# Queries and keys of an attention stage rotated by pairs of heads, transposed raw and split into high and low afterwards, with three of the four query pairs moved into the attention loop

## The chip, the cores and the metric

The kernel runs on one core of a Trainium2 chip. Five engines work side by side, each from its own queue and in the order of that queue: TensorE (PE in the profile; its weight loads are PEld), VectorE (DVE), ScalarE (ACT), GpSimd (POOL) and SyncE (SP), which only starts transfers. An engine that needs something from another waits on a semaphore, and everything behind the waiting instruction in its queue waits with it. The metric is the device time of one execution in microseconds (us).

## The reference

The reference is one encoder layer in float32, applied to two sequences of 512 tokens and 1024 channels. Each sequence goes through a feed-forward half step, a mixing block, and a second feed-forward half step. What matters here is the attention within the mixing block: 8 query heads of 64 channels share 2 key and value heads. Queries and keys are normalized per head, rotated by position in pairs of neighbouring channels, and used for a full softmax over the 512 tokens.

```python
aq = apply_rope(rms_norm(aq.reshape(B, S, ATT_HEADS, ATT_HEAD_DIM), q_norm), cos, sin)
ak = apply_rope(rms_norm(ak.reshape(B, S, ATT_KV_HEADS, ATT_HEAD_DIM), k_norm), cos, sin)

def apply_rope(x, cos, sin):
    x0, x1 = xf[..., 0], xf[..., 1]
    out = jnp.stack([x0 * c - x1 * s, x0 * s + x1 * c], axis=-1)

s = jnp.einsum('bqkgd,bskd->bkgqs', qi, k) * scale
p = jax.nn.softmax(s, axis=-1)
o = jnp.einsum('bkgqs,bskd->bqkgd', p, v)
```

Beside the attention the block computes a bidirectional chunkwise mLSTM memory and several sigmoid gates, all from one input projection.

## The kernel before

**High and low.** Every matmul works on pairs of float32r tiles: a value x is split into a high part (a copy rounded by ACT) and a low part (x minus the high part, by DVE). A projection is then three products (high by high, high by low, low by high). An attention score of one head over 64 channels is two products: the query tile holds the 64 high rows in one half of the 128 partitions and the 64 low rows in the other, and the key tile holds the high rows twice for the first product and the low rows twice for the second.

**The mixing block** is the generator `mix(s, ...)`, run once for each sequence, s = 0 and s = 1; the steps of the two are interleaved. In the profiled execution the part before the attention of s = 0 ends near 710 us and its attention loop lies at 710 to 830 us; the part before the attention of s = 1 is at 1020 to 1065 us and its loop at about 1090 to 1200 us. Tiles are tokens by channels until they are transposed: 4 blocks of 128 tokens stand side by side in a 128 x 512 tile.

**Before the attention.** `kv_done` normalizes and rotates the keys (`rope_apply`, L823 on: a product with the inverse root n, a product with the cosines o, products of the swapped neighbours with the sines m, and the sum). It splits them into `kst`, and `k_turn` transposes `kst` in 4 groups of 4 blocks. `q_done` leaves the raw queries of the 4 token blocks in four tiles. `q_rope(b)` does one token block with all its 8 heads: 4 DVE operations of 128 x 512, the split in two halves, 8 transposes of 128 x 128, and ACT copies into `qT` (heads by tokens). All four token blocks are done before the loop.

**The attention loop** (from L1112) runs over the heads h = 0 to 7 and, within a head, over b = 0 to 3. One step (h, b) puts on PE: the score of the next head for query block b (`score`, 2 matmuls); 5 filler matmuls of the gate projections (`among(FILLER[0])`); `turn_keys(Ps, b)`, which transposes key block b of the four probability tiles (4 transposes); 3 more filler matmuls; and `values` for the step before (2 matmuls). For each score DVE takes the row maximum (L1042), ACT the exponential (L1044), DVE the reciprocal (L1045), and either engine scales the tile (L1049 on DVE, L1047 on ACT). For each `turn_keys` ACT copies the high part out of PSUM and DVE forms the low part (`split`, L673 and L674); DVE's low part is the last reader of that bank.

**PSUM.** `PT()` hands out the two banks that the names pst belong to, in turn. Every transposing group of the mixing block takes one: `turn_keys`, the statistics of the other sequence (`col_sums`, L202, and its spreading, L212), and the turns of keys and queries. A group can start only when the last reader of the group two before it is done. Scores use two other banks (pss), fillers three (mm), values one (pso).

**Order.** Instructions wrapped in `pin` keep the order in which they are written; this holds for the scores, the transposes and values of the loop and for its fillers. All others are placed by a scheduling layer, and `shifted(n)` moves them in its order. While s = 0 runs, weights are fetched and split by ACT and DVE (`split_w`, L238 and L239, 128 x 1024 each) and also stored; for s = 1 they are loaded already split. The gate projections that serve as fillers end in a DVE product with the spread inverse root and an ACT tanh (`att_gate`, L1100 and L1101; `out_gate`, L974 and on).

Of the kernel before, what the change touches and what calls it, by code (L numbers as in the profile page):

```python
# [26 lines left out]
def encoder(ctx, tc, I, outs):  # L27
# [768 lines left out]
    def mix(s, xh, xl, early=None, extra=None, after=None):  # L796
# [26 lines left out]
        def rope_apply(t, rq, tab, bsel):  # L823

            cg, sg = tab
            if bsel is None:
                nb, cb, sb = 4, cg.unsqueeze(2).to_broadcast([P, 4, 2, DA]), sg
            else:
                nb, cb, sb = 1, cg[:, bsel].unsqueeze(1).to_broadcast([P, 8, DA]).unsqueeze(1), sg[:, bsel:bsel + 1]
            hn_ = 8 // nb  # L830
            n = T2()
            V_.tensor_tensor(n.rearrange("p (h e) -> p h e", e=DA), t.rearrange("p (h e) -> p h e", e=DA),
                             rq.unsqueeze(2).to_broadcast([P, 8, DA]), op=ALU.mult)
            o, m = T2(), T2()
            v4 = lambda x: x.rearrange("p (b h e) -> p b h e", b=nb, e=DA)
            V_.tensor_tensor(v4(o), v4(n), cb, op=ALU.mult)
            v5 = lambda x: x.rearrange("p (b h i two) -> p b h i two", b=nb, h=hn_, two=2)
            s4 = sb.rearrange("p b (i two) -> p b i two", two=2)
            for bb in range(nb):
                V_.tensor_tensor(v5(m)[:, bb], v5(n)[:, bb, :, :, ::-1],  # L840
                                 s4[:, bb].unsqueeze(1).to_broadcast([P, hn_, DA // 2, 2]), op=ALU.mult)
            V_.tensor_tensor(o, o, m, op=ALU.add)
            return o

        qT = A([P, HA, S], F32R, "qT")
        kst = qT[:, 4:8, :].rearrange("p a (g j u e) -> p (a g) j u e", g=2, j=2, u=2)

        def kv_done(pk):
# [10 lines left out]
            ko = rope_apply(kraw, rstd_cols(ssk, 8, DA), tabs[1], None)  # L859
            ko3 = ko.rearrange("p (g e) -> p g e", e=DA)  # L860
            nc.scalar.activation(kst[:, :, 0, 0, :], ko3, AF.Copy)
            nc.scalar.activation(kst[:, :, 0, 1, :], ko3, AF.Copy)
            V_.tensor_tensor(kst[:, :, 1, 0, :], ko3, f(kst[:, :, 0, 0, :]), op=ALU.subtract)
            V_.tensor_tensor(kst[:, :, 1, 1, :], ko3, f(kst[:, :, 0, 1, :]), op=ALU.subtract)

        qraw, rq = [], []

# [238 lines left out]
        if not s:  # L1106
            fill(1)
# [680 lines left out]
```

## Time and profile before

| | |
|---|---|
| three runs, median | 2062.38 us (2060.41, 2062.38, 2063.18) |
| span of the profiled execution, first to last instruction | 2059.1 us |
| granted TensorE clock, mean | 0.999 |
| PE busy | 2047.3 us, 99% |
| PE weight loads busy | 1691.3 us, 82% |
| DVE busy | 1553.0 us, 75% |
| ACT busy | 913.0 us, 44% |
| POOL busy | 92.8 us, 5% |
| chain of work that ended last | PE 97%, DVE 1%, ACT 1%, DMA 1% |

Of the profiled execution only the span is given, 3.3 us below the median of the three runs; no total time of its own stands beside it. A row of the timeline reads: start, duration, engine, line, operation, tile written <- tiles read, shape, how often, and in brackets the idle time of that engine before it with what ended it. Several like instructions in a row share a line (x2, x8). A duration on DVE or ACT is longer than the distance to the next start, since neighbours overlap a little: 128 x 512 operations of DVE last 0.69 us and start every 0.60 us when nothing holds them.

### The profile page before, as it was taken

How to read it: one execution, taken by the hardware profiler on the slowest of the kernel's cores; microseconds unless marked ns; L12 is line 12 of the kernel's file. 1: busy time of each engine (PE TensorE's matmuls, PEld its weight loads, DVE VectorE, ACT ScalarE, POOL GpSimd, SP SyncE). 2: the span in 40 equal slices, each digit the busy share in tenths (PEclk: the TensorE clock that was granted, in tenths of full speed). 3: DMA queues.
4: the chain of work that ended last, by engine and by line, in shares of the span. 5: the costliest groups of instructions: out<-in, count | busy, mean ns of one | idle time of the engine just before them, and what ended most of it. 6: DMA issues, size and time to landing. Idle time of an engine off the chain costs nothing.

```text
span 2059.1 us, 27038 instructions
## 1 busy us (share of the span) xinstructions
PE 2047.3 (99%) x9445; PEld 1691.3 (82%) x9445; DVE 1553.0 (75%) x2764; ACT 913.0 (44%) x1667; POOL 92.8 (5%) x108
## 2 busy tenths in 40 slices
PE   9999999999999999999999999999999999999998
PEld 7888888888888888888888888888888888888887
DVE  8888889886797787675566756455788888796797
ACT  7544444442235567563334553324544444443224
POOL 0000000001003000100120000001000000000001
PEclk9999999999999999999999999999999999999999
DMA  9656556799766753877684345677656555599753
GB/s 321 198 170 221 177 191 205 243 349 348 260 227 247 223 187 130 278 259 242 197 310 160 109 140 200 196 265 239 202 175 202 194 174 184 186 342 347 276 202 119
DMA packets 311015, 457.97 MB, mean 222 GB/s; under 512 B 20232, under 2 KB 182112, under 8 KB 309600
## 3 DMA queue, kind: packets, MB, share of 16 engines
q1 hardware_dynamic: 308800, 450.27, 64.6%
q0 software_dynamic: 1920, 5.72, 0.9%
q8 instruction: 74, 1.21, 0.2%
q14 instruction: 61, 0.50, 0.1%
q10 hardware_dynamic: 160, 0.27, 0.0%
HBM read 288.25 MB, written 167.94 MB: 222 GB/s over the span
## 4 chain that ended last, share of the span: by engine, by line
PE 97%; DVE 1%; ACT 1%; DMA 1%; issue 0%; SPq 0%; ACTq 0%; DVEq 0%
PE mm L789 15%; PE pso L332 12%; PE pst L332 12%; PE mm L332 10%; PE mm L590 8%; PE pss L332 6%; PE mm L776 6%; PE pst L590 4%; PE pss L590 4%; PE mm L756 4%; PE pso L590 3%; PE pso L1066 1%; PE pss L1039 1%; PE pst L1055 1%; PE pso L1235 1%; PE pss L1185 1%
## 5 line engine op out<-in xcount | busy, mean ns | idle before, releaser
L332 PE MATMUL pst<-xc,w 128*128 128x512 f32 x1056 | 253.6, 389 | 0.0
L332 PEld LDWEIGHTS pst<-xc,w 128*128 128x128 f32 x1056 | 198.3, 188 | 41.1
L332 PE MATMUL mm<-xc,w 128*128 128x512 f32 x972 | 229.9, 390 | 0.2 <-ACT f L340 0.2
L332 PEld LDWEIGHTS mm<-xc,w 128*128 128x128 f32 x972 | 181.9, 188 | 38.1 <-ACT f L340 0.6
L590 PE MATMUL mm<-rt,w 128*128 128x512 f32 x765 | 178.9, 389 | 0.0
L789 PE MATMUL mm<-xh,w 128*128 128x512 f32 x560 | 177.6, 393 | 0.0
L590 PEld LDWEIGHTS mm<-rt,w 128*128 128x128 f32 x765 | 143.6, 188 | 29.8
L290 ACT ACTIVATE w<-t 128x512 fp32r<-128x512 f32 x176 | 106.5, 627 | 135.7 <-issue 63.1
L291 DVE TENSOR_TENSOR w<-t,w 128x512 fp32r<-128x512 f32 x176 | 117.8, 688 | 47.9 <-ACT w L290 46.6
L332 PE MATMUL pss<-xc,w 128*128 128x512 f32 x528 | 126.8, 389 | 0.0
L332 PE MATMUL pso<-xc,w 128*128 128x512 f32 x528 | 126.8, 389 | 0.0
L332 PE MATMUL pso<-xc,f 128*128 128x512 f32 x528 | 126.8, 389 | 0.0
L789 PEld LDWEIGHTS mm<-xh,w 128*128 128x128 f32 x560 | 104.7, 188 | 21.2 <-DVE w L239 0.2
L332 PEld LDWEIGHTS pss<-xc,w 128*128 128x128 f32 x528 | 99.2, 188 | 20.5
L332 PEld LDWEIGHTS pso<-xc,w 128*128 128x128 f32 x528 | 99.1, 188 | 20.5
L332 PEld LDWEIGHTS pso<-xc,f 128*128 128x128 f32 x528 | 99.1, 188 | 20.5
L776 PE MATMUL mm<-xh,w 128*128 128x512 f32 x336 | 114.5, 401 | 0.0
L789 PE MATMUL mm<-xl,w 128*128 128x512 f32 x280 | 109.7, 392 | 0.0
L673 ACT ACTIVATE w<-wr 128x512 fp32r<-128x512 f32 x72 | 45.1, 632 | 137.0 <-PE pso L590 71.4
L673 ACT ACTIVATE w<-t 128x512 fp32r<-128x512 f32 x82 | 51.8, 632 | 107.4 <-PE pst L590 62.4
L590 PE MATMUL pst<-rt,w 128*128 128x512 f32 x396 | 93.7, 389 | 0.0
L590 PE MATMUL pss<-rt,w 128*128 128x512 f32 x396 | 93.7, 389 | 0.0
(407 smaller groups left out, 4037.5 us busy)
## 6 DMA issues: line engine op xcount, KB each, us to landing
rt<-rbuf SPq DMA_DIRECT2D x154, 512.0 KB, 5.7
wpark<-w SPq DMA_DIRECT2D x104, 512.0 KB, 3.4
w<-wpark SPq DMA_DIRECT2D x104, 512.0 KB, 4.8
wr<-in_ffn_w_gate_dram SPq DMA_DIRECT2D x62, 512.0 KB, 5.3
rbuf<-tab SPq DMA_DIRECT2D x102, 256.0 KB, 3.9
wr<-in_ffn_w_up_dram SPq DMA_DIRECT2D x44, 512.0 KB, 4.5
rbuf<-f SPq DMA_DIRECT2D x72, 256.0 KB, 4.1
wr<-in_w_in_dram SPq DMA_DIRECT2D x36, 512.0 KB, 5.7
```

Source lines behind the costliest of these rows:

```text
L290: pin(nc.scalar.activation(t[:, 0], src, AF.Copy))
L291: pin(V_.tensor_tensor(t[:, 1], src, f(t[:, 0]), op=ALU.subtract))
L332: nc.tensor.matmul(p, a[:, k, :], xt[:, b, k, :], start=(first and k == 0 and i == 0), stop=(k == HK_ - 1 and i == 2), skip_group_check=True)
L590: nc.tensor.matmul(p, u[:, a, d * P:(d + 1) * P], r[:, b, ts], start=(first and q == 0 and k == 0), stop=(q == len(us) - 1 and k == 2), sk ...
L673: nc.scalar.activation(hi, src, AF.Copy)
L756: nc.tensor.matmul(p[b][:, :N], a[:, k, bs], w_[:, kl, :], start=(k == 0 and i == 0), stop=(k == KD - 1 and i == 2))
L776: pin(nc.tensor.matmul(p[0], a[:, k, :], b, start=(k == 0 and i == 0), stop=(k == n - 1 and i == 2)))
L789: nc.tensor.matmul(p, a[:, k, :], b, start=(k == 0 and i == 0), stop=(k == n - 1 and i == 2))
L1039: pin(nc.tensor.matmul(p, qT[:, h, b * P:(b + 1) * P], kv[:, hk * 2 + j, :], start=(j == 0), stop=(j == 1)))
L1055: pin(nc.tensor.transpose(p[:, b * P:(b + 1) * P], Ps[b][:, kb * P:(kb + 1) * P], ident))
L1066: pin(nc.tensor.matmul(pos[h], Vst[:, kb, h // 4, :], w, start=(kb == 0 and i == 0), stop=(kb == 3 and i == 1)))
L1185: nc.tensor.matmul(p, qk[a][:, isl], qk[b], start=(n == 0), stop=(n == 2))
```

## The change

The rotation now works on a pair of heads for all four token blocks at once (a tile of 4 blocks by 128 channels). The pair is transposed as it is, unsplit, in one group of 4 (`pair_turn`), which gives both heads' 64 channels on the two halves of the partitions with all 512 tokens. The split comes after that, out of PSUM: for each head ACT copies the high half and DVE writes the low half to the other partitions, 64 x 512 each. For the keys one such group serves both heads. `kst`, its copies and its low parts go, and so do the splits of the queries in front of their transposes.

Per sequence PE transposes 4 blocks for the keys instead of 16, and 16 for the queries instead of 32. Over both sequences PE has 56 matmul instructions fewer (9377 for 9433), ACT 20 activations fewer, DVE 8 tensor operations more: the product with the sines is now two instructions of 256 columns in place of one of 512. Transfers and POOL's instructions are the same in number.

Query pair 1 (heads 0 and 1) is done before the loop. Pairs 2 to 4 are rotated at the loop's steps (0,0), (2,0) and (3,2) and turned at (0,2), (2,2) and (4,2), there pinned after the values and ahead of the next score. The raw queries wait in the upper half of `mg`, the tile that later takes the gates of the attention; the gates 4 to 7 of `att_gate` therefore come after the two `out_gate` units. `gate_tops` comes after the first pair's turn.

DVE in the loop of s = 0, from the low part of the turn of step (1,3) to that of step (2,1). The rows before (asm are the row statistics of a score, t2 the probability tiles and their parts, f2 and att the attention's output, pso the values, pst the turns):

```order
L674 TENSOR_TENSOR t2_591_6323<-pst_589_6317,t2_590_6322 128x512
L1045 RECIPROCAL asm_593_6334<-asm_593_6334 128x1
L1049 TENSOR_SCALAR t2_594_6336<-t2_594_6336,asm_593_6334 128x512
L674 TENSOR_TENSOR t2_597_6351<-pst_595_6345,t2_596_6350 128x512
L1042 TENSOR_REDUCE asm_600_6367<-pss_599_6364 128x1
L1078 TENSOR_TENSOR f2_567_6231<-pso_575_6261,f2_598_6359 64x512
L1045 RECIPROCAL asm_600_6367<-asm_600_6367 128x1
L674 TENSOR_TENSOR att_501_5939<-f2_567_6231,att_501_5939 128x512
L1042 TENSOR_REDUCE asm_607_6396<-pss_606_6393 128x1
L674 TENSOR_TENSOR t2_604_6384<-pst_602_6378,t2_603_6383 128x512
```

The same place now, in two pieces: from the low part of pst_562 (step (1,3)) to that of pst_571 (step (2,0)), and from there to that of pst_578 (step (2,1)). Lines of the attention loop are 11 lower than before: the turn of probabilities, L1055 before, is L1044 now, and L1055 is now the values.

```order
L674 TENSOR_TENSOR t2_564_6236<-pst_562_6230,t2_563_6235 128x512
L828 TENSOR_TENSOR t2_565_6244<-mg_373_5284,rs_439_5649 128x512
L830 TENSOR_TENSOR t2_566_6245<-t2_565_6244,tab_301_4209 128x512
L834 TENSOR_TENSOR t2_567_6246<-t2_565_6244,tab_301_4209 128x4x64 x2
L1067 TENSOR_TENSOR f2_540_6144<-pso_548_6174,f2_574_6280 64x512
L835 TENSOR_TENSOR t2_566_6245<-t2_566_6245,t2_567_6246 128x512
L1034 RECIPROCAL asm_569_6255<-asm_569_6255 128x1
L674 TENSOR_TENSOR t2_573_6272<-pst_571_6266,t2_572_6271 128x512
```

```order
L1038 TENSOR_SCALAR t2_570_6257<-t2_570_6257,asm_569_6255 128x512
L674 TENSOR_TENSOR att_471_5836<-f2_540_6144,att_471_5836 128x512
L1031 TENSOR_REDUCE asm_576_6288<-pss_575_6285 128x1
L980 TENSOR_TENSOR qT_372_5283<-pst_582_6314,qT_372_5283 64x512
L1031 TENSOR_REDUCE asm_584_6326<-pss_583_6323 128x1
L1034 RECIPROCAL asm_576_6288<-asm_576_6288 128x1
L968 TENSOR_TENSOR box_368_5279<-mm_561_6228,R_355_5156 128x512
L239 TENSOR_TENSOR w_587_6340<-wr_586_6338,w_587_6340 128x1024
L674 TENSOR_TENSOR t2_580_6305<-pst_578_6299,t2_579_6304 128x512
```

Between the first of these low parts and the third stood 8 instructions; now there are 16, among them the rotation's five (L828 to L835), the low half of a query (L980), a second row maximum and a weight split of 128 x 1024 (L239).

PE at step (2,2), before: the values of step (2,0), the next score, fillers, and the turn of this step. No other group uses the pst banks between the turn of step (2,1) and this one.

```order
L1066 MATMUL pso_605_6390<-t2_596_6350,kv_369_5280 128x512
L1066 MATMUL pso_605_6390<-t2_597_6351,kv_369_5280 128x512
L1039 MATMUL pss_606_6393<-kv_369_5280,qT_372_5283 128x512 x2
L776 MATMUL mm_588_6315<-xh_329_4889,w_561_6209 128x512 x2
L776 MATMUL mm_588_6315<-xl_330_4890,w_561_6209 128x512
L776 MATMUL mm_588_6315<-xh_329_4889,w_561_6209 128x512
L776 MATMUL mm_612_6416<-xh_329_4889,w_586_6309 128x512
L1055 MATMUL pst_613_6418<-ident_87,t2_559_6197 128x128
```

And now:

```order
L1055 MATMUL pso_581_6311<-t2_572_6271,kv_369_5280 128x512
L1055 MATMUL pso_581_6311<-t2_573_6272,kv_369_5280 128x512
L841 MATMUL pst_582_6314<-ident_87,t2_566_6245 128x128 x4
L1028 MATMUL pss_583_6323<-kv_369_5280,qT_372_5283 128x512 x2
L776 MATMUL mm_561_6228<-xh_329_4889,w_534_6122 128x512 x2
L776 MATMUL mm_561_6228<-xl_330_4890,w_534_6122 128x512
L776 MATMUL mm_561_6228<-xh_329_4889,w_534_6122 128x512
L776 MATMUL mm_589_6346<-xh_329_4889,w_559_6222 128x512
L1044 MATMUL pst_590_6348<-ident_87,t2_532_6110 128x128
```

The pair's turn pst_582 stands between two turns of probabilities, pst_578 and pst_590. With two banks in turn, pst_582 takes the bank of pst_571 and pst_590 that of pst_578, the group just before the pair's; before, pst_613 took the bank of the group two steps back.

The diff:

```diff
-        def rope_apply(t, rq, tab, bsel):
+        def rope_apply(t, rq, tab):
...
+            n, o, m = T2(), T2(), T2()
+            v4 = lambda x: x.rearrange("p (b h e) -> p b h e", b=4, e=DA)
+            V_.tensor_tensor(v4(n), t.rearrange("p b (h e) -> p b h e", e=DA),
+                             rq.unsqueeze(3).to_broadcast([P, 4, 2, DA]), op=ALU.mult)
+            V_.tensor_tensor(v4(o), v4(n), cg.unsqueeze(2).to_broadcast([P, 4, 2, DA]), op=ALU.mult)
+            v5 = lambda x: x.rearrange("p (b h i two) -> p b h i two", b=4, h=2, two=2)
+            s4 = sg.rearrange("p b (i two) -> p b i two", two=2)
+            for h in range(2):
+                V_.tensor_tensor(v5(m)[:, :, h], v5(n)[:, :, h, :, ::-1], s4, op=ALU.mult)
             V_.tensor_tensor(o, o, m, op=ALU.add)
             return o
 
+        def pair_turn(o, keep):
+            p = PT()
+            for b in range(4):
+                keep(nc.tensor.transpose(p[:, b * P:(b + 1) * P], o[:, b * P:(b + 1) * P], ident))
+            return p
...
         def k_turn():
-            for hk in range(HK):
-                for j in range(2):
-                    p = PT()
-                    for b in range(4):
-                        nc.tensor.transpose(p[:, b * P:(b + 1) * P],
-                                            f(kst[:, b * HK + hk, j]).rearrange("p a e -> p (a e)"), ident)
-                    nc.scalar.activation(kv[:, hk * 2 + j, :], p, AF.Copy)
+            p = pair_turn(kturned.pop(), lambda i: i)
+            for hk, own, other in ((0, lower, upper), (1, upper, lower)):
+                hi, lo = kv[:, hk * 2, :], kv[:, hk * 2 + 1, :]
+                nc.scalar.activation(hi[own, :], p[own, :], AF.Copy)
+                V_.tensor_tensor(lo[own, :], p[own, :], f(hi[own, :]), op=ALU.subtract)
+                nc.scalar.activation(hi[other, :], p[own, :], AF.Copy)
+                V_.tensor_tensor(lo[other, :], p[own, :], f(hi[own, :]), op=ALU.subtract)
...
-        def q_rope(b):
-            qo = rope_apply(qraw[b], rq[0][:, b * 8:(b + 1) * 8], tabs[0], b).rearrange("p (h e) -> p h e", e=DA)
-            for g in range(2):
-                qs = T2(F32R).rearrange("p (h u e) -> p h u e", u=2, e=DA)
-                split(qo[:, g * 4:g * 4 + 4], qs[:, :, 0, :], qs[:, :, 1, :])
...
+        def q_rope(pr):
+            return rope_apply(qraw[:, :, pr * P:(pr + 1) * P], rq[0][:, :, 2 * pr:2 * pr + 2], tabs[0])
+
+        def q_turn(pr, o, keep):
+            p = pair_turn(o, keep)
+            for h, own, other in ((2 * pr, lower, upper), (2 * pr + 1, upper, lower)):
+                nc.scalar.activation(qT[own, h, :], p[own, :], AF.Copy)
+                V_.tensor_tensor(qT[other, h, :], p[own, :], f(qT[own, h, :]), op=ALU.subtract)
...
-        for b in range(4):
-            q_rope(b)
-            if b == 0:
-                gate_tops(*tops)
+        q_turn(0, q_rope(0), lambda i: i)
+        gate_tops(*tops)
...
-        queue.extend(att_gate(d) for d in range(KD))
+        queue.extend(att_gate(d) for d in range(4))
         queue.extend(out_gate(h) for h in range(2))
+        queue.extend(att_gate(d) for d in range(4, KD))
...
             for b in range(4):
+                if (h, b) in ((0, 0), (2, 0), (3, 2)):
+                    qo = q_rope((h + 1) // 2 + 1)
+                if h in (0, 2, 4) and b == 2:
+                    q_turn(h // 2 + 1, qo, pin)
                 if h + 1 < HA:
                     nxt.append(score(h + 1, b))
```

More of the change, by code (lines that the diff above doesn't have):

```diff
@@ L848, in kv_done @@
+        lower, upper = slice(0, DA), slice(DA, P)
+        kturned = []
         def kv_done(pk):
@@ L1094, in among @@
                 between.pop(0)()
-        mg = A([P, KD, S], F32, "mg")
         def att_gate(d):
```

41 lines of the change are left out of this document (6 added, 35 removed).

## The prediction

> **What bounds the kernel now.** I read the page first (busy shares, chain), then busy time in windows around the two attention stages, then the timelines of PE and DVE within them.
>
> ```profile
> span 2059.1 us, 27038 instructions
> ...
> PE 2047.3 (99%) x9445; PEld 1691.3 (82%) x9445; DVE 1553.0 (75%) x2764; ACT 913.0 (44%) x1667; POOL 92.8 (5%) x108
> ...
> PE 97%; DVE 1%; ACT 1%; DMA 1%; issue 0%; SPq 0%; ACTq 0%; DVEq 0%
> ```
>
> ```profile
> 680.00:712.00 32.00, 31.77 (x170) 25.92 (x169) 28.89 (x67) 18.77 (x35) 0.00 (x0) 1.00 0.56 176
> 740.00:770.00 30.00, 30.00 (x154) 24.54 (x153) 25.95 (x59) 21.35 (x44) 0.00 (x0) 1.00 0.59 179
> 1020.00:1065.00 45.00, 44.30 (x224) 36.32 (x223) 35.73 (x74) 23.85 (x41) 7.05 (x8) 1.00 0.73 241
> 1125.00:1155.00 30.00, 30.00 (x155) 24.82 (x154) 24.21 (x57) 15.60 (x35) 0.00 (x0) 1.00 0.32 108
> ```
>
> A window row gives its length, then the busy time of PE, PEld, DVE, ACT and POOL, the clock, and the transfers. PE sets the time: work taken from its queue shortens the run, and every wait that it gains lengthens it. Within both loops (740 to 770, 1125 to 1155) PE never stops, but DVE is busy 25.95 of 30 us and 24.21 of 30 us. There is room on DVE, not much, and PE consumes what DVE makes within a step or two. The times before are 2062.38 us in the median; the execution that the rows come from spans 2059.1 us, 3.3 us under it. I make the sum in differences and set it against the median.
>
> **What goes: 56 transposes.** Their price is the distance from start to start, not the duration.
>
> ```profile
> 683.38 1.19 PE L882 MATMUL pst<-ident,qT 128*128 128x128 f32 x8
> ...
> 684.88 0.60 PE L882 MATMUL pst<-ident,qT 128*128 128x128 f32 x4
> 685.23 0.47 PE L789 MATMUL mm<-xl,w 128*128 128x512 f32 x1
> 685.54 0.39 PE L789 MATMUL mm<-xh,w 128*128 128x512 f32 x1
> 685.77 0.60 PE L882 MATMUL pst<-ident,qT 128*128 128x128 f32 x4
> ...
> 704.62 1.06 PE L987 MATMUL pst<-ident,t 128*128 128x128 f32 x8
> 705.44 0.48 PE L789 MATMUL mm<-xh,w 128*128 128x512 f32 x1
> 705.76 0.39 PE L789 MATMUL mm<-xl,w 128*128 128x512 f32 x1
> ...
> 709.64 0.39 PE L1039 MATMUL pss<-kv,qT 128*128 128x512 f32 x1
> ```
>
> Four transposes take 685.23 - 684.88 = 0.35 us, and the matmul behind them starts its successor 0.31 us later, where an ordinary one does so after 0.23 (685.54 to 685.77). A group of 4 thus costs 0.35 + 0.08 = 0.43 us, a group of 8 costs 0.82 + 0.09 = 0.91. Before, a sequence has for the keys one group of 8 and two of 4 (0.91 + 0.87 = 1.78 us) and for the queries four of 8 (3.64); now it has five groups of 4 (2.17). That is 3.25 us a sequence, 6.5 us in all. The Trainium skill (page "TensorE: Matmul & The Clock Gate", section "Back-to-back issue gap") gives about 81 ns for one matmul of 128 columns in a sustained stream; as an estimate 56 of them would be 4.5 us, and the forecast 2.0 us later. This trace shows 0.82 / 8 = 0.10 us each for float32 transposes, and I keep its price.
>
> With them go the waits that stand in front of these groups: PE is idle 32.00 - 31.77 = 0.23 us and 45.00 - 44.30 = 0.70 us in the two windows before the loops, and in the new order the groups that waited there for the splits are gone. I take all 0.9 us; the other end is 0. The gain is 7.4 us.
>
> **What is neutral.** ACT's 20 activations fewer: it is busy 18.77 of 32 us there, and PE does not wait for its sum. The key chain after the turn (ACT, DVE, ACT, DVE, 0.6 to 0.7 us each, under 3 us) is covered by fillers: more than 20 us of matmuls stand between the key turn (683.38) and the first score (709.64). In s = 1 the new `qT` takes a buffer whose last reader is the last matmul of the output projection of s = 0, so the first query copy waits for that; 48 matmuls (11 us at 0.23) still stand between it and the first score, against the same 3 us chain. Transfers and POOL keep their counts. If that cover fails, this wait costs up to its 3 us; I take 0.
>
> **What is new: the ropes on DVE in the loop.** One rotation is n, o, two halves of m, and the sum.
>
> ```profile
> L674 DVE TENSOR_TENSOR t<-t,t 128x256 fp32r<-128x256 f32 x8 | 3.0, 420 | 0.0
> L842 DVE TENSOR_TENSOR t<-t,t 128x512 f32<-128x512 f32 x4 | 2.7, 686 | 0.0
> L1078 DVE TENSOR_TENSOR f<-pso,f 64x512 f32<-64x512 f32 x8 | 5.5, 685 | 0.1
> ```
>
> ```profile
> 745.96 1.22 DVE L239 TENSOR_TENSOR w<-wr,w 128x1024 fp32r<-128x1024 f32 x1 [0.79 <-ACT w L238]
> ...
> 747.10 0.68 DVE L1042 TENSOR_REDUCE asm<-pss 128x1 f32<-128x512 f32 x1
> 747.70 0.68 DVE L674 TENSOR_TENSOR t<-pst,t 128x512 fp32r<-128x512 f32 x1
> ...
> 749.24 0.68 DVE L674 TENSOR_TENSOR t<-pst,t 128x512 fp32r<-128x512 f32 x1
> ...
> 753.65 0.68 DVE L674 TENSOR_TENSOR t<-pst,t 128x512 fp32r<-128x512 f32 x1
> ```
>
> From start to start a 512-column operation takes 0.60 us (747.10 to 747.70) and 256 columns, by the same subtraction, 0.33; L239 takes 1.14. A rotation is 3 x 0.60 + 2 x 0.33 = 2.5 us, a query pair's two low parts another 1.2. So 3.7 us of DVE are added to each of three places per loop, in the time of two or three steps of 3.2 us. The place decides. PE at the second place of s = 0, and one row of the mechanism that matters:
>
> ```profile
> 750.78 0.60 PE L1055 MATMUL pst<-ident,t 128*128 128x128 f32 x4
> 753.98 0.60 PE L1055 MATMUL pst<-ident,t 128*128 128x128 f32 x4
> 755.59 0.60 PE L202 MATMUL pst<-ident,R 128*128 128x128 f32 x4
> 757.41 0.40 PE L776 MATMUL mm<-xh,w 128*128 128x512 f32 x1
> 757.80 0.66 PE L1055 MATMUL pst<-ident,t 128*128 128x128 f32 x4
> ...
> 757.06 0.68 DVE L674 TENSOR_TENSOR t<-pst,t 128x512 fp32r<-128x512 f32 x1
> ```
>
> The turn at 757.80 should have come 0.23 us after 757.41, at 757.64; it waited until the low part of the turn before it ended (757.06 + 0.68). The reason is the statistics group at 755.59: a third group on two banks, so that the next turn needs the bank of its immediate predecessor. `q_turn` is such a group, three times a loop. The Trainium skill (page "Perfetto Trace Analysis", section "Matmuls") wants independent groups to rotate through PSUM banks so that one's evacuation overlaps the next; here the extra group shortens that rotation, and 757.80 shows the price when DVE is late.
>
> *Second pair, s = 0, the largest term.* I walk DVE's new order from 745.96: L239 to 747.10, row maximum to 747.70, low part of (1,3) to 748.3, n, o, m, m to 750.15, L1067 to 750.75, the sum to 751.35, reciprocal 0.15, low part of (2,0) to 752.2 (before: 749.84), scale 0.4, att's low part, row maximum, a query low part, row maximum (0.6 each) to 755.0, reciprocal, gate product to 755.65, L239 to 756.8, low part of (2,1) to 757.5. PE reaches the turn of (2,2) at 753.98, plus 0.43 for the pair's group and 0.2 for the values that wait for 752.2: 754.6. It needs the bank of (2,1), free at 757.5: 2.9 us idle. With the 0.2 at the values that is 3.1; the 0.16 us of 757.80 go, since DVE has caught up.
>
> *First and third pair, s = 0.* At (0,0) the scale that the first turn needs moves behind n and o:
>
> ```profile
> 722.16 0.49 DVE L1049 TENSOR_SCALAR t<-t,asm 128x512 f32<-128x512 f32 x1
> ...
> 722.31 0.73 PE L1055 MATMUL pst<-ident,t 128*128 128x128 f32 x4
> ...
> 765.81 1.23 DVE L239 TENSOR_TENSOR w<-wr,w 128x1024 fp32r<-128x1024 f32 x1 [0.40 <-ACT w L238]
> ...
> 771.13 0.60 PE L1055 MATMUL pst<-ident,t 128*128 128x128 f32 x4
> ```
>
> That scale ended at 722.65 and PE's fourth transpose is already held to it; one operation of 0.60 more makes 0.55 us. At (3,2) DVE runs from 765.81 without a gap through L239, row maximum, low part, n, o, m, m, L218, sum, reciprocal and low part: 1.14 + 7 x 0.60 + 2 x 0.33 + 0.15, and 0.09 for the end of the last, 6.24 us, to 772.05, where PE wants that bank at 771.13: 0.9. The next head's first turn then waits some 0.5 for its last scale. Sum for s = 0: 0.55 + 3.1 - 0.16 + 0.9 + 0.5 = 4.9 us.
>
> *s = 1.* Here no weights are split, and DVE waits about once a step.
>
> ```profile
> 1124.54 0.69 DVE L674 TENSOR_TENSOR t<-pst,t 128x512 fp32r<-128x512 f32 x1
> ...
> 1127.07 0.16 DVE L1045 RECIPROCAL asm<-asm 128x1 f32<-128x1 f32 x1 [0.85 <-ACT t L1044]
> ...
> 1132.87 0.60 PE L1055 MATMUL pst<-ident,t 128*128 128x128 f32 x4
> ...
> 1134.48 0.60 PE L202 MATMUL pst<-ident,R 128*128 128x128 f32 x4
> ```
>
> The rotation fills such gaps. At (0,0) everything still meets PE. From 1124.54 the same walk puts the low part of (2,1) at 1133.6 and the second query low part at 1136.0. PE comes to the turn of (2,2) at 1132.87 + 0.43 = 1133.3 (0.35 us idle) and to the statistics, which need the bank of the pair's group, at 1134.48 + 0.8 = 1135.3 (0.75). At (3,2) it is 0.1. Sum 1.2 us.
>
> **Sum.** -7.4 + 4.9 + 1.2 = -1.3 us: 2062.38 - 1.3 = 2061.1. The new waits' ends: 0, if the ropes' lateness is absorbed, and twice the 6.1, since each walk starts on a row that ACT or a transfer could also delay. Less than about 0.2% (4.1 us) cannot be told from no change here.
>
> **Rivals.**
> *DVE covers the ropes.* For it: 30.00 - 25.95 = 4 us are free in the fullest window, and an order that looks bad by hand costs nothing if the rows ahead come early. Against it: 757.80, where one extra group already held PE. With waits of at most 2 us: 2062.4 - 7.4 + 1 = 2056.
> *ACT and DVE wait for each other, and the kernel is slower.* The query parts alternate between the two engines in order, ACT's second copy standing behind a probability scale that needs DVE's reciprocal. Each crossing has a price in the rows: 0.85 us before the reciprocal at 1127.07, 0.40 before L239. If each of the six pair turns pays one such crossing in PE time beyond my walk, 6 x 0.9 = 5.4 us come on top: 2066.5. It is slower than before from 0.22 us a turn (1.3 / 6), by more than 0.2% from 0.9.
> *The transposes were not on PE's path.* Then nothing is gained and 6.1 us are lost: 2068.5. Against it PE's 97% of the chain.
>
> **How the numbers follow.** The forecast's own case, 2058.3 to 2064.5, has 0.49; covered ropes, 2055 to 2058.3, 0.20; mutual waits, 2064.5 to 2068.5, 0.25; transposes off the path or worse, 0.06. The range 2056 to 2068 leaves out about 0.15. Faster by over 0.2% (under 2058.3) is the covered case, 0.20. Slower by over 0.2% (over 2066.5) is some two thirds of the mutual waits and the last case, 0.23. Within: 0.57.
>
> **What would show it.** PE matmuls 56 fewer; PE idle in the windows of the loops, which is 0 now: some 5 us in that of s = 0 and 1.2 in that of s = 1, ended by DVE's low part (L674) in front of L1044, the largest near (2,2) of s = 0. If PE has no gap there, the covered case holds; if gaps stand in front of scores (L1028) and end on ACT or on L980, the mutual waits do. A gap in front of the first scores of s = 1 would mean that the buffer of `qT` was not covered.

## The result and the profile after

The changed kernel takes 2068.77 us in the median of five runs (2065.74 to 2069.39), the kernel before 2062.21 us in the same measurement (2060.39 to 2063.18). The ratio is 1.0032, with a 95% interval of 1.0020 to 1.0044: slower by 6.6 us, where 1.3 us less was predicted. Here and below, single executions that took over 200 us longer at a lower granted clock (0.56 to 0.85) are left out of medians, ranges and ratios.

The page of the changed kernel, with the lines that answer to the first ones shown of before:

```profile
span 2063.9 us, 26903 instructions
...
PE 2044.1 (99%) x9389; PEld 1685.3 (82%) x9389; DVE 1559.3 (76%) x2772; ACT 905.3 (44%) x1647; POOL 93.1 (5%) x108
...
PE 93%; DVE 4%; DMA 1%; ACT 1%; issue 0%; SPq 0%; DVEq 0%; ACTq 0%
```

PE has 56 instructions (9389 for 9445; the trace counts 12 more in each kernel than the part on the change does) and 3.2 us of busy time less, the span is 4.8 us longer, and DVE's share of the chain has gone from 1% to 4%. PE waits more than it saves. The windows that were shown of before:

```profile
680.00:712.00 32.00, 31.45 (x150) 25.73 (x149) 26.46 (x64) 15.89 (x28) 0.00 (x0) 1.00 0.68 222
740.00:770.00 30.00, 26.68 (x137) 21.54 (x136) 27.10 (x58) 18.82 (x36) 0.00 (x0) 1.00 0.45 150
1020.00:1065.00 45.00, 43.90 (x203) 35.79 (x202) 26.25 (x57) 15.82 (x24) 8.29 (x9) 1.00 0.73 235
1125.00:1155.00 30.00, 28.33 (x147) 22.85 (x146) 27.56 (x64) 14.85 (x33) 0.00 (x0) 1.00 0.32 106
```

In the loops PE is now idle for 3.3 of 30 us in s = 0 and for 1.7 of 30 us in s = 1; it was idle for nothing. In the windows ahead of the loops its idle time did not go but grew, from 0.23 to 0.55 us and from 0.70 to 1.10. The view of waits sums, for PE, what it waited for (total, times, longest, in us):

```profile
PE pst L1044 <- DVE t L674: 3.7, 2, 3.0
...
PE pst L841 <- DVE t L835: 1.6, 2, 1.1
PE pst L1044 <- ACT t L1036: 1.2, 1, 1.2
PE pst L202 <- DVE qT L980: 1.0, 1, 1.0
...
PE mm L789 <- DMA w<-wpark: 0.4, 1, 0.4
PE mm L789 <- DVE w L239: 0.4, 1, 0.4
```

L1044 is the turn of the probabilities, L841 the turn of a pair, L202 the statistics group. In the timeline of PE the larger of these waits, in order:

```profile
698.41 0.66 PE L841 MATMUL pst<-ident,t 128*128 128x128 f32 x4 [0.56 <-DVE t L835]
...
755.57 0.63 PE L1044 MATMUL pst<-ident,t 128*128 128x128 f32 x4 [2.98 <-DVE t L674]
...
777.44 0.33 PE L1044 MATMUL pst<-ident,t 128*128 128x128 f32 x1 [1.25 <-ACT t L1036]
...
1050.17 0.66 PE L841 MATMUL pst<-ident,t 128*128 128x128 f32 x4 [1.05 <-DVE t L835]
...
1135.90 0.63 PE L1044 MATMUL pst<-ident,t 128*128 128x128 f32 x4 [0.70 <-DVE t L674]
...
1138.65 0.63 PE L202 MATMUL pst<-ident,R 128*128 128x128 f32 x4 [0.97 <-DVE qT L980]
```

A sum of waits does not say where a lead over the old kernel was won or lost. For that I matched the 8722 matmuls that are not transposes, which both traces have in the same sequence of work, and took for each its start now minus its start before. How this offset changes over a stage is what the stage cost. The predicted column is the prediction's own terms put into the same stages: ahead of a loop 1.78 + 3.64 - 2 x 0.43 = 4.56 us of transposes less and the old wait (0.23 or 0.70), in a loop 3 x 0.43 us of turns and the new waits (4.9 or 1.2).

| stage | predicted, us | measured, us |
|---|---|---|
| start of the execution to 680 us | 0 | +0.7 |
| ahead of the loop, s = 0 | -4.8 | -4.5 |
| loop, s = 0 | +6.2 | +7.2 |
| ahead of the loop, s = 1 | -5.3 | -4.0 |
| projections behind that, waits for weights | 0 | +1.2 |
| loop, s = 1 | +2.5 | +4.0 |
| rest | 0 | +0.2 |
| sum | -1.4 | +4.8 |

The sum is that of the two profiled spans, 2063.9 - 2059.1. Between the medians it is 6.6; the first experiment shows where most of the rest lies. The first row has nothing to do with the change: over the profiles of all runs below, in which the work up to there is the same, it lies between -0.2 and +2.6 us. So single profiles are compared stage by stage here, and times by their medians.

### The profile page after: what moved, and what is told of

Read it like the earlier page. It is cut to its first block, busy times and chain, and to the rows that moved or that the text cites. A ratio compares the mean times of both kernels' runs of the same rounds, so it can differ in the third digit from the quotient of the medians.

```text
span 2063.9 us, 26903 instructions
## 1 busy us (share of the span) xinstructions
PE 2044.1 (99%) x9389; PEld 1685.3 (82%) x9389; DVE 1559.3 (76%) x2772; ACT 905.3 (44%) x1647; POOL 93.1 (5%) x108
## 4 chain that ended last, share of the span: by engine, by line
PE 93%; DVE 4%; DMA 1%; ACT 1%; issue 0%; SPq 0%; DVEq 0%; ACTq 0%
PE mm L789 14%; PE pso L332 12%; PE pst L332 12%; PE mm L332 11%; PE mm L590 8%; PE pss L332 6%; PE pst L590 4%; PE pss L590 4%; PE mm L776 4%; PE mm L756 4%; PE pso L590 3%; PE pso L1055 1%; PE pso L1227 1%; PE pst L1044 1%; PE pss L1177 1%; PE pso L756 1%
```

## Experiments

The theory is that DVE is late at single places: each new wait is one DVE operation that ends after PE wants it, at a place where the order puts a whole rotation (a rope, 2.5 us) ahead of it. The main rivals are that DVE's total work in the loop counts, wherever it stands, and that the work ahead of the loops is where the time is lost.

### The changed kernel again

> The changed kernel once more, unchanged. Its profiled execution showed a granted clock of 1.00 throughout and took 2065.7 us, while its other executions took up to 2069.4. Clock theory: in those the gap of about 3 us in front of the turn at (2,2) of s = 0 is followed by a stretch at half clock, as the run with the ropes on GpSimd showed behind a gap of 4 us (6.5 us long, some 3.2 us lost). Then executions fall into two groups, near 2065.7 and near 2068.8, and a profiled one of the upper group shows PEclk 0.5 in some 6 us behind that gap. Rival: the spread is that of the start of the run and of transfers, times lie evenly between 2065 and 2069, and the clock is 1.00 whatever the time.

2068.50 us in the median (2066.99 to 2070.82), 1.0032 [1.0022, 1.0043]. This time the profiled execution took 2069.01 us. The same wait in it, and then three windows (length, busy PE, PEld, DVE, ACT, POOL, clock, transfers):

```profile
756.14 0.63 PE L1044 MATMUL pst<-ident,t 128*128 128x128 f32 x4 [2.99 <-DVE t L674]
```

```profile
757.00:759.00 2.00, 2.00 (x8) 1.57 (x8) 1.59 (x3) 0.54 (x2) 0.00 (x0) 0.52 0.93 258
759.00:761.00 2.00, 2.00 (x8) 1.62 (x7) 1.44 (x4) 0.03 (x1) 0.00 (x0) 0.62 0.36 125
761.00:763.00 2.00, 2.00 (x12) 1.65 (x11) 1.72 (x9) 1.71 (x4) 0.00 (x0) 1.00 0.00 0
```

Some 0.9 us after PE has started again its clock is halved for some 3.5 us (a window that it fills only in part shows a mean, 0.52 or 0.62): 8 matmuls fit into 2 us instead of 12. Matched with the first profiled execution, the matmuls lose 1.6 us over this stretch (the offset goes from 0.57 to 2.15 us). In that first execution a wait of 2.98 us in the same place left the clock alone:

```profile
757.00:759.00 2.00, 2.00 (x12) 1.67 (x11) 1.97 (x4) 0.00 (x0) 0.00 (x0) 1.00 0.93 273
```

A third execution with this gap, that of the run with the first pair's turn later, has the half clock right behind a gap of 2.98 us that ends at 754.90:

```profile
755.00:757.00 2.00, 2.00 (x7) 1.78 (x8) 1.94 (x5) 1.42 (x4) 0.00 (x0) 0.50 0.97 286
```

So a gap of 3.0 us halves the clock in some executions and not in others. The Trainium skill (page "TensorE: Matmul & The Clock Gate", section "What's actually happening") has the clock fall after an idle window of about 3.4 us, and the window runs freely and does not start anew with the kernel; that a gap of 3.0 us decides now one way and now the other agrees with a window whose phase changes. That the whole window has to be idle is not borne out: here 3.0 us are enough, and another run below shows less. The expected two groups of times were not there: the times lie spread between 2065.7 and 2070.8, and the second profiled execution has some 1.7 us more from other places, such as a wait of 0.8 us at 846 us that the first doesn't show. In an execution in which the clock falls, that makes up 1.6 of the 1.8 us that the medians are further apart than the profiled spans. In how many of the executions without a profile it falls is not shown: their mean clocks (0.997 to 0.999) differ by little more than such a stretch is worth.

### The turn of a pair in another pool's bank

```diff
         def pair_turn(o, keep):
-            p = PT()
+            p = (MM if keep is pin else PT)()
```

> The three pair turns of the loop take one of the three filler banks (mm) in place of one of the two pst banks; nothing else moves. Theory A (the ropes' time on VectorE makes its low parts late, whichever bank the turn takes): the gap of 3.0 us before the turn of step (2,2) of s = 0 goes only in part; about 2 us reappear in front of the values (L1055), which wait for the same low part; the gap at the last scale of head 4 (1.2 us) stays; the waits of s = 1 at L1044 and L202 (0.7 and 1.0) go. About 3 us less than the changed kernel's 2068.8: 2065.5. Theory B (the bank is the cause): all gaps at L1044 ended by L674 and the one at L202 go and none appears in their place: 4.7 us less, 2064 or under. If fillers then wait for their bank, the time is above either.

2063.32 us (2061.98 to 2065.41), 1.0009 [0.9999, 1.0018]: 5.4 us less than the changed kernel, the time of theory B. The turns in the loop no longer use the two pst banks, so that a turn of the probabilities does not need the bank of its immediate predecessor. PE then reaches step (2,2) without the gap of 3 us, but the late parts of the probabilities are met a few matmuls further, by the values, as theory A has it:

```profile
754.09 0.50 PE L1055 MATMUL pso<-t,kv 128*128 128x512 f32 x1 [0.87 <-ACT t L673]
754.97 0.51 PE L1055 MATMUL pso<-t,kv 128*128 128x512 f32 x1 [0.38 <-DVE t L674]
```

1.25 us in place of 2.98: the bank carried more than half of the price, and DVE's lateness is below it. With two short gaps in place of a long one the clock is not halved anywhere in the loops of its profile, and its mean is 0.999 or 1.000 in every execution; the changed kernel's is 0.997 to 0.999. By the matched matmuls the loops cost 1.1 and 1.2 us less than in the changed kernel; a half clock that no longer comes would add 1.6 us, and the rest of the 5.4 is not attributed.

### No rotation in the loop

```diff
-                if (h, b) in ((0, 0), (2, 0), (3, 2)):
-                    qo = q_rope((h + 1) // 2 + 1)
                 if h in (0, 2, 4) and b == 2:
-                    q_turn(h // 2 + 1, qo, pin)
+                    pr = h // 2 + 1
+                    q_turn(pr, qraw[:, :, pr * P:(pr + 1) * P], pin)
```

> Left out: the rotation of query pairs 2 to 4 (their raw queries are turned and split as they are), so that five VectorE operations fall away in six places; turns, banks, splits and order stay. Theory A (VectorE's added time): the new gaps in the two loops, 6 us in s = 0 and 2.5 us in s = 1, go nearly all, 7 us less than 2068.8: 2062. Theory B (bank alone): a gap of about 1 us or more stays before each turn that follows a pair's turn: 2065. Theory C (ScalarE and VectorE wait for each other over the query parts): most of the gaps stay, 2066 or more.

2061.88 us (2060.71 to 2064.01), 1.0000 [0.9990, 1.0009]. Query pairs 2 to 4 enter the scores unrotated, and nothing else is left out. The 15 DVE operations in a loop are worth 6.9 us, with the half clock behind the gap that they cause (the longest gap is 1.6 us here, and the clock stays at 1.00 in both loops). That is theory A's time. Without them, and with 56 transposes less, the kernel is still no faster than before. What is left is not in the rotation:

```profile
PE pst L202 <- DVE qT L981: 1.9, 2, 1.6
...
PE pst L841 <- DVE t L835: 1.6, 2, 1.1
...
PE mm L789 <- DMA w<-wpark: 0.8, 1, 0.8
```

The statistics group still needs the bank of the pair's turn and waits for its two low parts (L202), which is theory B's gap, but at one group only (1.6 us), and the waits ahead of the loops stand as they were.

### All four pairs before the loop

```diff
+        for pr in range(1, 4):
+            q_turn(pr, q_rope(pr), lambda i: i)
...
-                if (h, b) in ((0, 0), (2, 0), (3, 2)):
-                    qo = q_rope((h + 1) // 2 + 1)
-                if h in (0, 2, 4) and b == 2:
-                    q_turn(h // 2 + 1, qo, pin)
```

> All four pairs are rotated and turned before the loop; the loop has neither ropes nor pair turns. Theory A: the loops have no new gaps (8.5 us less), but VectorE, busy 26.5 of the 32 us before the loop of s = 0, gets 11 us more there and PE waits some 1 to 5 us in front of the first scores: 2061 to 2065. If VectorE's surplus is taken up by the loop's first steps: 2057 to 2060, the 6.5 us of the transposes come out in full.

2071.62 us (2069.67 to 2073.02), 1.0046 [1.0030, 1.0062], 6.6 us above the highest that was expected. The loops now cost what they cost before (the offset of the matched matmuls changes by less than 0.1 us over each), and all is lost ahead of them:

```profile
PE pst L841 <- DVE t L835: 3.5, 4, 1.5
PE mm L789 <- DMA w<-wpark: 3.2, 1, 3.2
PE mm L776 <- ACT w L238: 2.9, 1, 2.9
```

The last two of these waits cost more than they last. Behind the one of 2.9 us (to 715.73) and behind the one of 3.2 us (to 1086.99) the clock is halved, for 5.3 and 6.2 us of work:

```profile
716.00:720.00 4.00, 3.66 (x8) 2.38 (x9) 3.92 (x6) 1.87 (x3) 0.00 (x0) 0.50 0.81 325
```

The order of the kernel before did a quarter of the rotation at a time, by token block, between many other pieces. Four rotations in a row fill DVE (3.92 of 4 us in this window), and in s = 0 the ACT half of the weight split (L238) comes late because it stands in ACT's queue behind copies that wait for DVE. That the wait for weights from memory in s = 1 has the same cause is not shown.

### The rotation on GpSimd

```diff
-        def rope_apply(t, rq, tab):
+        def rope_apply(t, rq, tab, eng=None):
+            V_ = eng or nc.vector
...
+        qo = q_rope(1)
-                if (h, b) in ((0, 0), (2, 0), (3, 2)):
+                if (h, b) in ((1, 0), (3, 0)):
```

with `eng` set to GpSimd for pairs 2 to 4.

> The rotations of pairs 2 to 4 run on GpSimd, begun before the first scores, at step (1,0) and at step (3,0), eight steps ahead of their turns; turns, banks and splits as in the changed kernel. Theory A: as without the ropes, 7 us less than 2068.8: 2062, since GpSimd is idle there and has 10 us or more for 5 operations of about 1.5 us. If GpSimd's operations slow VectorE's (a 128x512 one now and then took 1.4 us in place of 0.69 while GpSimd was busy), part comes back: 2064 to 2067. Theory B: as for the run without ropes, 2065.

2074.12 us (2072.91 to 2075.83), 1.0060 [1.0042, 1.0078], the slowest, and 7 us above the highest that was expected. DVE has less to do but does it more slowly while POOL works. Timeline of DVE, then of POOL:

```profile
691.80 1.23 DVE L239 TENSOR_TENSOR w<-wr,w 128x1024 fp32r<-128x1024 f32 x1
...
694.40 2.31 DVE L239 TENSOR_TENSOR w<-wr,w 128x1024 fp32r<-128x1024 f32 x1
696.63 1.22 DVE L831 TENSOR_TENSOR t<-t,tab 128x512 f32<-128x512 f32 x1
697.78 2.34 DVE L835 TENSOR_TENSOR t<-t,tab 128x256 f32<-128x256 f32 x2
```

```profile
691.96 1.97 POOL L829 TENSOR_TENSOR t<-mg,rs 128x512 f32<-128x512 f32 x1 [29.32 <-ACT kv L878]
694.01 1.61 POOL L831 TENSOR_TENSOR t<-t,tab 128x512 f32<-128x512 f32 x1
695.59 2.85 POOL L835 TENSOR_TENSOR t<-t,tab 128x256 f32<-128x256 f32 x2
```

The same weight split takes 1.23 us where it starts ahead of POOL's product (691.80, as long as in the kernel before with POOL idle, 1.22 at 745.96) and 2.31 where POOL's product has started first (694.01). The Trainium skill (page "SBUF — State Buffer", section "SBUF: two separate sides") says that GpSimd and a DVE operation with two SBUF inputs take turns at one pair of ports, each for its whole instruction, the one that starts first ahead; the two times of the split agree. The pair-1 turn, which waits for these operations, comes 3.8 us late, and behind it the clock is halved for longer than above:

```profile
695.00:701.50 6.50, 2.70 (x12) 1.89 (x11) 6.42 (x6) 0.62 (x1) 4.76 (x4) 0.99 0.85 269
701.50:708.00 6.50, 6.50 (x18) 5.04 (x19) 4.18 (x14) 1.33 (x4) 0.00 (x0) 0.50 0.24 68
```

In the loop of s = 1 of this run the half clock follows two short waits close together:

```profile
1149.94 0.33 PE L1046 MATMUL pst<-ident,t 128*128 128x128 f32 x1 [1.06 <-DVE t L1040]
...
1151.70 0.66 PE L1057 MATMUL pso<-t,kv 128*128 128x512 f32 x1 [0.51 <-DVE t L674]
1152.16 1.05 PE L1030 MATMUL pss<-kv,qT 128*128 128x512 f32 x2
```

From 1152.16 two matmuls last 1.05 us instead of 0.62 to 0.71, for 3 us; the granted clock from 1152 to 1155 is 0.50.

### The first pair's turn later

```diff
-        q_turn(0, q_rope(0), lambda i: i)
+        qo = q_rope(0)
...
-        go(mem_qk(0, 1), mem_qk(1, 0), mem_qk(1, 1))
+        load, comp = mem_qk(1, 0)
+        go(mem_qk(0, 1), (load, lambda w: (q_turn(0, qo, lambda i: i), comp(w))), mem_qk(1, 1))
```

> Only the first query pair's turn moves: it is issued behind the next block of matmuls of the memory branch instead of ahead of the gates' top parts, with the same operations. DVE theory (each new wait is one DVE operation that is late at its place): the two waits on the rope's sum (L841 behind L835, 0.97 and 1.46 us over both sequences by the ledger) go, and 2.4 us with them; the median goes from 2068.8 to about 2066.4. Rival: the time in front of the first scores is bounded by the weights and the gates that DVE also splits, the wait only moves behind the turn, and the median stays within 0.5 us of 2068.8.

2067.57 us (2066.68 to 2069.95), 1.0028 [1.0018, 1.0038], where the changed kernel beside it took 2068.50, 1.0032 [1.0022, 1.0043]: 0.9 us less and not 2.4, and the intervals overlap, so a gain is not shown. The two waits on the rope's sum were 0.56 and 1.05 us by the rows above, 1.6 and not 2.4. In the view of waits PE no longer waits for that sum; the turn waits 0.5 us for another DVE result (L1014), which is 1.1 us won, and for weights, the next thing that is late, PE waits 2.4 us in place of 0.8 (0.4 and 0.4 above), which is more than was won. This is nearer to the rival:

```profile
PE mm L789 <- DVE w L239: 1.3, 2, 0.9
...
PE mm L789 <- DMA w<-wpark: 1.1, 1, 1.1
...
PE pst L841 <- DVE st L1014: 0.5, 1, 0.5
```

### Only the keys turned raw

The kernel before, with `kv_done` and `k_turn` of the changed one and nothing else.

> The kernel before with the keys alone changed: turned raw, four transposes instead of 16 a sequence, split behind the turn; the queries as before. Prediction: 1.78 - 0.43 = 1.35 us a sequence, 2.7 in all, nothing else: 2059.3. The ledger of the changed kernel shows -1.4 for s = 0 there. Rival: the key chain behind the turn is not covered, or the matmuls that follow wait elsewhere: no gain, 2062.

2063.38 us (2061.56 to 2064.41), 1.0004 [0.9995, 1.0014]; 2059.3 was expected, so the expectation missed. PE does 24 transposes less, and PE's offset falls ahead of the loops as it should, but it is given back completely at the queries' transposes, which still wait for the splits of all the rotated queries:

```profile
PE pst L1004 <- DVE t L674: 3.9, 4, 1.6
```

Before, this wait was 0.7 us. I read this so: in this stage PE was hardly ahead of DVE, and transposes taken from PE are worth something only if DVE's work there shrinks as well. With the keys alone DVE is still busy 28.24 us in the window of 32 (28.89 before), in the changed kernel 26.46, and there the gain was real. No run changes DVE's work alone there. The two halves of the change don't add.

### The second rope three steps earlier

```diff
-                if (h, b) in ((0, 0), (2, 0), (3, 2)):
+                if (h, b) in ((0, 0), (1, 1), (3, 2)):
```

> The changed kernel with the rope of pair 3 (heads 4 and 5) issued three steps earlier, at (1,1) instead of (2,0); the same operations, nothing else moved. DVE theory with the clock: in s = 0 the wait of 3.1 us at the turn of (2,2) goes, with it the stretch at half clock behind it (1.4 us), and in s = 1 the waits at (2,2) and the statistics (0.87 and 1.14); the rope now delays the low parts of (1,2) and (1,3) by some 1 us in each sequence. 2068.8 - 3.1 - 1.4 - 2.0 + 2.0 = 2064.3, and the granted clock is 1.00 all through. Rival: DVE is so full that five operations in one step cost the same anywhere: a wait of about 3 us turns up at (1,3) or (2,0), and the median stays at 2068.

2063.68 us (2062.90 to 2066.16), 1.0011 [1.0002, 1.0020]; 2064.3 was expected. One place in the source is worth 5.1 us. PE is idle 1.3 us in the window of s = 0 (3.3 before the edit) and 0.3 us in that of s = 1 (1.7), and the long wait has left the list, whose first line is now

```profile
PE pst L1044 <- ACT t L1036: 2.0, 2, 1.3
```

No stretch at half clock follows in its profile. That five operations cost the same wherever they stand is refuted.

### Three places

The same with the third rope at (3,1), the turns in the other pool's banks and the first pair's turn later.

> Ropes in one piece, as in the changed kernel, but the second at (1,1) and the third at (3,1), the turns in the other pool's banks, and the first pair's turn later. DVE theory: each of the waits named so far is met by one of the edits, but five operations still stand in one step three times a loop; some 1 us a rope is left (3 us a sequence less what the place hides): 2061 to 2063. Rival: in one piece the ropes cost as much as in turn_in_mm, 2063.3 less 2.4 for the first turn is the least, and nothing is won by the places: 2061 at best with no gap smaller. The run beside it, in which the operations stand apart, then shows nothing better.

2063.59 us (2063.24 to 2066.18), 1.0009 [1.0000, 1.0018], above the 2061 to 2063 expected: these edits, two of which gained over 5 us by themselves, gain no more together than the best of them. Its profile has no wait over 0.9 us in the attention stages; in the window of 740 to 770 PE is idle for 1.8 us, in several pieces. By the matched matmuls its two loops cost 8.3 us (11.2 in the changed kernel), of which 2.6 are the six turns. With the rope in one piece, some wait is left in each of the arrangements tried.

### The rope's operations one to a step

The first pair's turn later, the turns in the other pool's banks, and each rope taken into five pieces, worked in the tile of the raw queries with one temporary tile beside it:

```diff
+            return got, [n, lambda: m(0), lambda: m(1), o, add]
...
         for b in range(4):
             Ps.append(score(0, b))
+            if b:
+                ops[1][1].pop(0)()
...
-                if (h, b) in ((0, 0), (2, 0), (3, 2)):
-                    qo = q_rope((h + 1) // 2 + 1)
+                pr = 1 if h == 0 else 2 if 4 * h + b < 11 else 3
+                if ops[pr][1] and (h, b) not in ((0, 2), (0, 3), (2, 0), (2, 2)):
+                    ops[pr][1].pop(0)()
```

The diff is that of the last of three forms. In the first two the last piece of the third rope stands at (4,1); by then, in s = 0, a gate has overwritten the first token block of the raw queries, from which heads 6 and 7 are still to be formed. The number and the size of the operations are the same in all three.

> The first pair's turn as in the run beside it; the ropes of pairs 2 to 4 are taken apart, one of their five operations to a step of the loop instead of five in one step, worked in place with one temporary tile; their turns take the bank of another pool as in the run turn_in_mm. DVE theory: no step gets more than 0.6 us of DVE on top, so that of the loops' waits (5.9 and 2.7 us) most go. What remains is 56 transposes less, 6.5 us, with the old 0.9 of waits, against some 1.2 us of waits on weights and 1 to 2 us of rest: 2062 - 7.4 + 3 = 2057.6, below the kernel before. Rival: it is the sum of DVE's work in the loop that counts (25.95 of 30 us before, 3 x 3.7 us more), wherever it stands; then about as much is lost as with the ropes in one piece, 2063 to 2066.

> As the run spread, with the sum of each rope written to the temporary tile instead of back into the tile of the raw queries, whose first half is overwritten by a gate while the loop runs; the same operations on every engine. The rope's operations stand one to a step. DVE theory: as spread, 2060.7, since no engine does more or less; below the kernel before by 1.5 us. In the profile no wait of over 1.1 us in the loops and PEclk 1.00 throughout. Rival: the longer life of the temporary tile holds back the later ropes, 2062 or more.

> As spread_apart, with the third rope's operations at (2,3) to (3,3), so that its sum stands ahead of the gate that overwrites the raw queries; the first two ropes stand as they did. DVE theory: no step gets more than one operation of 0.6 us on top, nothing else changes: 2060.7, below the kernel before by 1.5 us and below the ropes in one piece at their best places (2063.6) by 2.9; PE idle in the loop of s = 0 some 2 us. Rival: the third rope now falls on the steps where the second pair's low parts are made, and up to 1 us comes back at (2,3) to (3,1): 2061.7.

The first form takes 2060.70 us (2059.56 to 2063.43), 0.9995 [0.9985, 1.0004], where 2057.6 was expected; the second 2060.73, 0.9994 [0.9985, 1.0003]; the third, whose ropes are whole, 2059.69 us (2058.54 to 2062.07) where the kernel before took 2062.77 beside it, 0.9988 [0.9979, 0.9997]. The third form is 9 us faster than the changed kernel with as many instructions on PE, DVE and ACT, and a little faster than the kernel before. The 9 us are those of several edits together. What the spreading is worth by itself the run with three places tells, which has the same banks and the same first turn: 3.9 us (2063.59 and 2059.69), and 2.9 us with the second form, measured beside it. The matched matmuls give the same, 4.6 us for the two loops in place of 8.3. The windows of the third form:

```profile
740.00:770.00 30.00, 29.44 (x153) 23.94 (x152) 27.59 (x61) 20.29 (x40) 0.00 (x0) 1.00 0.54 175
...
1125.00:1155.00 30.00, 30.00 (x158) 24.59 (x157) 27.17 (x64) 16.75 (x37) 0.00 (x0) 1.00 0.32 106
```

DVE is as busy as in the changed kernel (27.59 us for 27.10, 27.17 for 27.56) and a little busier than with three places (26.79 and 26.31), and PE is idle 0.6 us for 3.3 and 0 for 1.7. So it is not the sum of DVE's work that held PE. Two waits for weights (L239, 1.3 us) remain in front of the loop of s = 1, the largest of what the change still costs.

## Why the prediction was wrong

**Gain of 56 transposes (6.5 us): right where DVE gets out of the way.** Ahead of the loop of s = 0 the offset falls by 4.5 us, and with the operations spread the kernel ends 2.3 us ahead of the one before by the matched matmuls. The rival in which the transposes were not on PE's path is refuted.

**"The groups that waited there for the splits are gone. I take all 0.9 us": the step that failed first.** The groups went, but the turn of pair 1 stands in their place and waits for a rope that is one operation longer and comes in one piece: PE is idle 0.56 and 1.05 us in front of it (698.41 and 1050.17), where the prediction has 0. I had counted the idle time of windows without walking DVE's new order there, as I did in the loop. Ahead of the two loops the forecast is missed by 1.6 us (0.3 and 1.3). It is the first of several steps that failed, and none alone carries the 6.2 us by which the table misses: 1.2 us are weights, 2.5 us the loops' waits, which were taken too small (4.9 and 1.2 us for 5.9 and 2.7), 0.9 us lie outside these stages, and the clock comes on top.

**No wait for weights: not a term.** Some 1.2 us are lost behind the first stage of s = 1, where PE's lead meets weights that come no earlier than before; with the turn of pair 1 moved away this wait is longer (2.4 us in the view for 0.8).

**Second pair, s = 0 (2.9 us and 0.2 at the values): right in place, cause and size.** PE waits 2.98 us at the turn of (2,2) for the low part of (2,1), and 0.34 at the values, which also wait for a low part. DVE's rows in the changed kernel:

```profile
745.64 0.68 DVE L828 TENSOR_TENSOR t<-mg,rs 128x512 f32<-128x512 f32 x1
...
749.28 0.69 DVE L674 TENSOR_TENSOR t<-pst,t 128x512 fp32r<-128x512 f32 x1
...
754.74 0.68 DVE L674 TENSOR_TENSOR t<-pst,t 128x512 fp32r<-128x512 f32 x1
```

The walk put 9.2 us from the first of these (748.3) to the end of the last (757.5); they are 9.8 us apart. The trace has both earlier, as PE leads by about 2.6 us there by the matched matmuls; that lead shifts the turn as well, so the wait keeps its size.

**First and third pair, s = 0:** 0.4 us at (0,0) for 0.55 predicted; the 0.9 us at (3,3) didn't come; the scale for head 4, taken at 0.5 and on DVE, cost 1.5 us and ends on ACT (777.44). An exponential ahead of it on ACT had waited for a row maximum that stood behind the rope on DVE:

```profile
774.57 0.69 ACT L1033 ACTIVATE t<-pss,asm 128x512 f32<-128x512 f32 x1 [2.88 <-DVE asm L1031]
```

The loop's waits are 5.9 us by the matched matmuls (7.2 - 3 x 0.43) for 4.9.

**s = 1 (1.2 us): right in place, less than half the size.** By the matched matmuls the turn of (2,2) costs 0.9 us for 0.35 predicted, the statistics 1.1 for 0.75, and some 0.7 us lie at places the walk had as meeting PE: 2.7 us.

**The clock was taken at 1.00.** A predicted gap of 3 us was not asked for what it does to PE's clock. Its fall is worth some 1.6 us in the executions in which it comes, and brings the 4.8 us of the spans to 6.4, near the 6.6 us of the medians. How often it comes in executions without a profile is not shown, and those of one kernel differ by more than what is left.

**The rivals.** That ACT and DVE wait for each other gave a time near the one measured, 2066.5, but for another reason: of its six crossings one shows (777.44), which begins with the rope on DVE, and the runs put the loss on DVE's lateness at two banks, on the rope ahead of the loop and on the clock. The 0.7 us by which the execution was later at 680 us lies ahead of any edit.

## What to carry to other kernels

When work moves from one stage to another, walk the new order of the engine that makes the data in every stage that the change touches, the one that gets lighter too: what replaces the removed group has a producer of its own. Spread a block of operations over the steps of a pipelined loop, one to a step: here the same operations cost 3 to 4 us less so than in one piece at the best places found, with the producer just as busy. Treat a predicted gap of 3 us on PE as two costs, the gap and a stretch at half clock.

## What was unexpected of the hardware

A single gap of 3.0 us on PE (2.99) was followed by some 3.5 us at half clock (8 matmuls in 2 us for 12) in one execution and by none (2.98) in another; after the turn that came 3.8 us late it was 6.5 us at 0.50. Single gaps of 1.6 us left the clock alone (the rotation left out, only the keys), but gaps of 1.06 and 0.51 us that ended within 2 us of each other were followed by 3 us at 0.50 in one run. And a DVE product of 128 x 1024 with both inputs in SBUF took 2.31 us for 1.23 when a product on GpSimd had started just ahead of it.
